# Feature-major k, q and v projections: one 512-column operand instead of three 256-column matmuls, with the halves added when a chunk is emptied

## The chip, the cores and the metric

One Trainium2 chip, of which one core runs the whole program. The metric is the device time of one execution in microseconds (us), from the timed runs of the unchanged kernel and of the changed one.

## What is computed

The reference is one decoder block for 256 tokens of width 2048 in float32. Cut to what matters here:

```python
h = _rms_norm(x, attn_norm)
proj = h @ w_in                      # NSA q, kv, gates | GDN q, k, v | z | a | b | merge gates
o_a = _nsa_mixer(...)                # attention branch
pad = jnp.pad(qkv, ((0, 0), (3, 0), (0, 0)))
conv = sum(conv_w[i] * pad[:, i:i + S_] for i in range(4))
conv = jax.nn.silu(conv)             # then q, k, v of the gated delta rule
o_b = _gated_delta_chunked(...)
x = x + (sigmoid(m_a) * (o_a @ w_branch_a) + sigmoid(m_b) * (o_b @ w_branch_b)) @ w_out
x = x + SwiGLU(_rms_norm(x, ffn_norm))
```

The change touches the product of `h` with the 6144 columns of `w_in` that give q, k and v of the gated delta rule, and the convolution that reads them.

## The kernel before, in words

Every large product is computed from split operands: a float32 number is written as a high part (rounded to the PE's float32r format) and a low part (the remainder), and a product is the sum high·high + high·low + low·high. Activations are split once and kept in SBUF (`hT_hi`, `hT_lo`: the normalised input, transposed, 16 k-tiles of 128 features by 256 tokens). Weights are streamed: `load_pair` (lines 99 to 111) loads two k-tiles by 512 columns with one DMA on SP's queue into `raw`, ScalarE (ACT) makes the high part `whi` (line 107), VectorE (DVE) makes the low part `wlo` (line 108). There are four `raw` buffers and three each of `whi` and `wlo`.

There are two kinds of chunk, each 512 weight columns wide and eight pairs of k-tiles long. A token-major chunk (`chunk_tok`, lines 113 to 128) holds the activations as the stationary operand and moves the 512 weight columns: three matmuls of 512 columns for each k-tile and each half of the tokens (lines 122 to 124), into two PSUM banks. A feature-major chunk (`chunk_feat`, lines 130 to 146) holds 128 of the weight columns as the stationary operand and moves the 256 tokens: for each of 16 k-tiles and each of four column blocks `s` it issues three matmuls of 256 columns (lines 141 to 143), and two column blocks share one PSUM bank, so that the chunk fills two banks. The pool `psm` has four banks with the tag `mm`, so that a chunk of either kind can begin while the one before it is being emptied.

The gated delta rule goes over four groups of four heads (`gdn_group`). Each group runs the k, the q and the v chunk feature-major and then the gate chunk z token-major; after the first two groups a merge-gate chunk follows, and two more come after the fourth. So there are 12 feature-major chunks. When one ends, `conv_silu` (lines 645 to 657) empties it: for each column block ScalarE scales PSUM by the last filter tap (line 651) and VectorE adds the other three taps, reading PSUM three times (line 654). What follows for a group (norms, the products of k with k and q, the inverse of a triangular block matrix, the recurrence, the output norm) is cut into small steps in a queue of side tasks, and two steps are recorded after each pair of k-tiles of the running chunk. The inverse is a serial chain on VectorE (lines 786 and 789, 31 rounds) followed by two round trips through DRAM (`ud<-xl`, `U<-ud`) to the matmuls at line 805. The last steps of the last group are recorded when the first two chunks of the product with `w_branch_b` have come as far as they can without them (`run_pair`).

That is the recorded order. The order in which each engine runs its instructions is then set when the program is built, by a scheduler that may move independent instructions past each other; on the chip each engine takes its list in order.

## Time and profile before

| what | value |
|---|---|
| timed runs (3) | median 1974.73 us, 1974.52 to 1977.64 |
| span of the profiled execution, first to last instruction | 1971.1 us (its whole time is not listed apart; the median of the timed runs is 3.6 us above the span) |
| TensorE (PE) | 99% of the span busy, 10485 matmuls |
| VectorE / ScalarE | 59% / 47% busy |
| DMA | 367 MB, 186 GB/s on average |
| stage of the gated delta rule, where the change lies | about 518 to 1085 us of the span |

How to read it: times are microseconds from the first instruction unless marked ns. A matmul's record lasts from its issue to its modelled end, and the next one begins before it ends, so the pace of the PE is the distance between the starts, not the length of a record. PEld is the weight load that goes with each matmul. The granted clock of the PE is 1.00 at 2.4 GHz and 0.50 at 1.2 GHz. A side matmul in plain float32 shows as two records. A releaser is what ended an engine's wait.

### The profile page before, as it was taken

The numbers are of one execution on the slowest core, as the hardware profiler recorded it, in microseconds if no ns is written. First come the engines' busy times: TensorE is split into PE (matmuls) and PEld (weight loads), VectorE is DVE, ScalarE is ACT, GpSimd is POOL, SyncE is SP. The second block draws the span as 40 slices with busy tenths as digits, with TensorE's granted clock in tenths as the row PEclk, the third lists the DMA queues.
The fourth block names the chain that finished last, engine by engine and source line by source line (L and its number), as shares of the span: only waits on it lengthen the run. The fifth ranks groups of instructions, "written<-read, shape, count | busy, mean of one in ns | idle before, by whom it ended". The sixth has DMA issues, their size and how long they took to land.

```text
span 1971.1 us, 27260 instructions
## 1 busy us (share of the span) xinstructions
PE 1946.4 (99%) x10485; PEld 1651.0 (84%) x10485; DVE 1155.0 (59%) x1715; ACT 928.4 (47%) x1377; POOL 54.1 (3%) x97
## 2 busy tenths in 40 slices
PE   8999999999999999999999999999999999999999
PEld 6878877876998998999987788888888888888887
DVE  5555766655468587687774665554455444544443
ACT  5434555555454554654543544444444444443333
POOL 0001000001000000100100000000000000000000
PEclk9999999999999999999999999999999999999999
DMA  8566545546767566566574965666666666656663
GB/s 231 170 183 193 161 129 162 170 149 200 217 173 203 169 178 198 158 193 166 153 200 157 333 201 183 191 192 183 191 191 186 191 191 191 191 185 201 201 202 130
DMA packets 207605, 367.04 MB, mean 186 GB/s; under 512 B 25473, under 2 KB 34546, under 8 KB 207090
## 3 DMA queue, kind: packets, MB, share of 16 engines
q1 hardware_dynamic: 207442, 365.28, 62.1%
q8 instruction: 82, 1.34, 0.3%
q14 instruction: 49, 0.40, 0.1%
q10 hardware_dynamic: 32, 0.01, 0.0%
HBM read 355.76 MB, written 9.45 MB: 185 GB/s over the span
## 4 chain that ended last, share of the span: by engine, by line
PE 96%; DMA 2%; DVE 1%; ACT 0%; SPq 0%; issue 0%; POOL 0%; ACTq 0%; POOLq 0%; DVEq 0%
PE mm L123 25%; PE mm L124 24%; PE mm L122 24%; PE mm L141 4%; PE mm L143 4%; PE mm L142 4%; PE sd L183 1%; PE sd L668 1%; PE sd L448 1%; PE sd L561 1%; DMA Q<-grow_d 1%; PE sd L748 1%; DMA raw<-in_w_branch_b_dram 1%; PE sd L567 1%; PE sd L568 0%; PE sd L267 0%
## 5 line engine op out<-in xcount | busy, mean ns | idle before, releaser
L108 DVE TENSOR_TENSOR wlo<-raw,whi 128x1024 fp32r<-128x1024 f32 x632 | 773.7, 1225 | 658.5 <-ACT whi L107 656.1
L107 ACT ACTIVATE whi<-raw 128x1024 fp32r<-128x1024 f32 x632 | 669.7, 1060 | 804.5 <-PE mm L124 674.4
L123 PE MATMUL mm<-wlo,hT_hi 128*128 128x512 f32 x704 | 276.7, 393 | 0.0
L124 PE MATMUL mm<-whi,hT_lo 128*128 128x512 f32 x704 | 276.5, 393 | 0.0
L124 PE MATMUL mm<-whi,h2T_lo 128*128 128x512 f32 x704 | 274.0, 389 | 0.0
L123 PE MATMUL mm<-wlo,h2T_hi 128*128 128x512 f32 x704 | 273.9, 389 | 0.0
L122 PE MATMUL mm<-whi,hT_hi 128*128 128x512 f32 x704 | 260.2, 393 | 0.0
L122 PE MATMUL mm<-whi,h2T_hi 128*128 128x512 f32 x704 | 249.9, 390 | 0.0
L143 PE MATMUL mm<-hT_hi,wlo 128*128 128x256 f32 x768 | 218.4, 285 | 0.0
L141 PE MATMUL mm<-hT_hi,whi 128*128 128x256 f32 x768 | 218.4, 285 | 0.0
L142 PE MATMUL mm<-hT_lo,whi 128*128 128x256 f32 x768 | 218.3, 284 | 0.0
L124 PEld LDWEIGHTS mm<-whi,hT_lo 128*128 128x128 f32 x704 | 132.3, 188 | 27.7 <-issue 1.1
L123 PEld LDWEIGHTS mm<-wlo,hT_hi 128*128 128x128 f32 x704 | 132.3, 188 | 27.5 <-issue 1.1
L124 PEld LDWEIGHTS mm<-whi,h2T_lo 128*128 128x128 f32 x704 | 132.2, 188 | 27.5
L122 PEld LDWEIGHTS mm<-whi,h2T_hi 128*128 128x128 f32 x704 | 132.2, 188 | 27.1
L123 PEld LDWEIGHTS mm<-wlo,h2T_hi 128*128 128x128 f32 x704 | 132.2, 188 | 27.0
L122 PEld LDWEIGHTS mm<-whi,hT_hi 128*128 128x128 f32 x704 | 132.1, 188 | 26.3 <-issue 0.2
L141 PEld LDWEIGHTS mm<-hT_hi,whi 128*128 128x128 f32 x768 | 147.2, 192 | 0.6
L142 PEld LDWEIGHTS mm<-hT_lo,whi 128*128 128x128 f32 x768 | 147.2, 192 | 0.2
L143 PEld LDWEIGHTS mm<-hT_hi,wlo 128*128 128x128 f32 x768 | 146.9, 192 | 0.4
L123 PE MATMUL mm<-wlo,act 128*128 128x512 f32 x352 | 138.5, 393 | 0.0
L124 PE MATMUL mm<-whi,act 128*128 128x512 f32 x352 | 138.4, 393 | 0.0
(288 smaller groups left out, 2247.7 us busy)
## 6 DMA issues: line engine op xcount, KB each, us to landing
raw<-in_w_in_dram SPq DMA_DIRECT2D x272, 512.0 KB, 3.7
raw<-in_w_gate_dram SPq DMA_DIRECT2D x88, 512.0 KB, 4.4
raw<-in_w_up_dram SPq DMA_DIRECT2D x88, 512.0 KB, 3.7
raw<-in_w_down_dram SPq DMA_DIRECT2D x88, 512.0 KB, 4.7
raw<-in_w_branch_a_dram SPq DMA_DIRECT2D x32, 512.0 KB, 4.7
raw<-in_w_branch_b_dram SPq DMA_DIRECT2D x32, 512.0 KB, 4.9
raw<-in_w_out_dram SPq DMA_DIRECT2D x32, 512.0 KB, 4.7
wc<-in_w_cmp_dram SPq DMA_DIRECT2D x16, 256.0 KB, 4.2
```

What stands on the lines that cost most here:

```text
L107: nc.scalar.activation(hi[:, :, :width], raw[:, :, :width], AF.Copy)
L108: nc.vector.tensor_tensor(lo[:, :, :width], raw[:, :, :width], hi[:, :, :width].bitcast(F32), ALU.subtract)
L122: nc.tensor.matmul(o, lhsT=sh, rhs=hi[:, j, :width], start=kt == 0, stop=False)
L123: nc.tensor.matmul(o, lhsT=sh, rhs=lo[:, j, :width], start=False, stop=False)
L124: nc.tensor.matmul(o, lhsT=sl, rhs=hi[:, j, :width], start=False, stop=kt == kts - 1)
L141: nc.tensor.matmul(o, lhsT=hi[:, j, ws], rhs=xh[:, kt, :], start=first, stop=False, skip_group_check=True)
L142: nc.tensor.matmul(o, lhsT=hi[:, j, ws], rhs=xl[:, kt, :], start=False, stop=False, skip_group_check=True)
L143: nc.tensor.matmul(o, lhsT=lo[:, j, ws], rhs=xh[:, kt, :], start=False, stop=last, skip_group_check=True)
L183: nc.tensor.transpose(pt[:, i * P : (i + 1) * P], s4, ident)
L448: nc.tensor.matmul(pc[:60, :P], lhsT=kp[:, l0 + l, :], rhs=wc[:, l, :], start=l0 + l == 0, stop=l0 + l == 31)
L561: nc.tensor.transpose(pt[:n, r * P : (r + 1) * P], pb[:, r, c0 : c0 + n], ident)
L567: nc.tensor.matmul(po, lhsT=wh, rhs=ph[:n], start=i == 0, stop=False)
```

## The change

The moving operand of a feature-major chunk becomes one access of 512 columns, the 256 tokens of the high part and then the 256 of the low part. For that the two halves of each large activation are put in one tile (`big_pair`: two buffers of the pool `big` instead of four of half the size). One matmul of 512 columns with the weight's high part now gives high·high in the first half of a PSUM bank and high·low in the second half, and one matmul of 256 columns adds low·high to the first half. A column block therefore takes a whole bank, and a chunk takes all four. When it is emptied, ScalarE copies the second half of each bank to a new tile `xs` in SBUF, VectorE adds the first half to it, and the convolution reads `xs` instead of PSUM. The other lines of the diff follow from the new tiles, or drop comments.

```diff
-    big = ctx.enter_context(tc.tile_pool(name="big", bufs=4))
+    big = ctx.enter_context(tc.tile_pool(name="big", bufs=2))
...
+    def big_pair(name):
+
+        b = big.tile([P, 2, KD, S], F32R, tag="big", name=nm(name))
+        return b, b[:, 0], b[:, 1]
...
-    def chunk_feat(w, c0, evac, xh, xl):
-        ps = [psm.tile([P, 512], F32, tag="mm", name=nm("mm")) for _ in range(2)]
+    def chunk_feat(w, c0, evac, xhl):
+
+        ps = [psm.tile([P, 512], F32, tag="mm", name=nm("mm")) for _ in range(4)]
...
+                first, last = kt == 0, kt == KD - 1
                 for s in range(4):
-                    o = ps[s // 2][:, (s % 2) * S : (s % 2 + 1) * S]
                     ws = slice(s * P, (s + 1) * P)
-                    first = kt == 0 and s % 2 == 0
-                    last = kt == KD - 1 and s % 2 == 1
-                    nc.tensor.matmul(o, lhsT=hi[:, j, ws], rhs=xh[:, kt, :], start=first, stop=False, skip_group_check=True)
-                    nc.tensor.matmul(o, lhsT=hi[:, j, ws], rhs=xl[:, kt, :], start=False, stop=False, skip_group_check=True)
-                    nc.tensor.matmul(o, lhsT=lo[:, j, ws], rhs=xh[:, kt, :], start=False, stop=last, skip_group_check=True)
+                    nc.tensor.matmul(
+                        ps[s].rearrange("p (q c) -> p q c", q=2), lhsT=hi[:, j, ws], rhs=xhl[:, :, kt, :],
+                        start=first, stop=False, skip_group_check=True,
+                    )
+                    nc.tensor.matmul(
+                        ps[s][:, :S], lhsT=lo[:, j, ws], rhs=xhl[:, 0, kt, :], start=False, stop=last, skip_group_check=True
+                    )
...
         ca = gdn.tile([P, 4, S], F32, tag="ca", name=nm("ca"), bufs=2)
+        xs = gdn.tile([P, 4, S], F32, tag="xs", name=nm("xs"), bufs=1)
         for s in range(4):
-            src = ps[s // 2][:, (s % 2) * S : (s % 2 + 1) * S]
+            nc.scalar.activation(xs[:, s, :], ps[s][:, S:], AF.Copy)
+            nc.vector.tensor_tensor(xs[:, s, :], ps[s][:, :S], xs[:, s, :], ALU.add)
+        for s in range(4):
+            src = xs[:, s, :]
             a = ca[:, s, :]
             nc.scalar.activation(a, src, AF.Copy, scale=conv_col(3, base + s))
```

The built programs are the same on every engine up to the first feature-major chunk, and from within the product with `w_branch_b` on. Between them the scheduler has set another order. Three places show it. Line numbers of the changed kernel are higher by two to six than those of the kernel before; `mm` is a PSUM bank of a chunk, `ca` the convolution's result.

The first turn from a k chunk to a q chunk (group 0) on ScalarE. Before:

```order
L107 ACTIVATE whi_4732<-raw_4730 128x1024
L107 ACTIVATE whi_4770<-raw_4768 128x1024
L651 ACTIVATE ca_4686<-mm_4413,cw_425 128x256
L107 ACTIVATE whi_4800<-raw_4798 128x1024
L651 ACTIVATE ca_4686<-mm_4414,cw_425 128x256
L651 ACTIVATE ca_4686<-mm_4413,cw_425 128x256
L107 ACTIVATE whi_4830<-raw_4828 128x1024
```

and now:

```order
L109 ACTIVATE whi_4678<-raw_4676 128x1024
L109 ACTIVATE whi_4708<-raw_4706 128x1024
L652 ACTIVATE xs_4622<-mm_4410 128x256
L652 ACTIVATE xs_4622<-mm_4411 128x256
L652 ACTIVATE xs_4622<-mm_4412 128x256
L109 ACTIVATE whi_4730<-raw_4728 128x1024
L652 ACTIVATE xs_4622<-mm_4413 128x256
L657 ACTIVATE ca_4621<-xs_4622,cw_423 128x256 x4
```

Two conversions for the next chunk (4678 and 4708) still stand ahead of the emptying; three of the four copies come before the third conversion.

The same turn on VectorE, now:

```order
L110 TENSOR_TENSOR wlo_4679<-raw_4676,whi_4678 128x1024
L110 TENSOR_TENSOR wlo_4709<-raw_4706,whi_4708 128x1024
L653 TENSOR_TENSOR xs_4622<-mm_4410,xs_4622 128x256
L653 TENSOR_TENSOR xs_4622<-mm_4411,xs_4622 128x256
L653 TENSOR_TENSOR xs_4622<-mm_4412,xs_4622 128x256
L110 TENSOR_TENSOR wlo_4731<-raw_4728,whi_4730 128x1024
L653 TENSOR_TENSOR xs_4622<-mm_4413,xs_4622 128x256
L660 SCALAR_TENSOR_TENSOR ca_4621<-xs_4622,cw_423,ca_4621 128x255 x3
```

The additions stand behind the conversion of the second pair of the q chunk, and three of the four ahead of the third pair's. On the PE the q chunk opens with the eight matmuls on its first bank for both of these pairs, and only then goes to the second bank. Most of the other q and v chunks open in the same way; at seven of the twelve turns out of a feature-major chunk, side matmuls stand at the boundary as well.

The end of the last group's side tasks, on the PE. `y` is the output of one half of the tokens, whose four transposes (line 668, now 674) end the work of that half; `mm` here are banks of the `w_branch_b` chunks. Before, around the first half's `y`:

```order
L124 MATMUL mm_10357<-whi_10450,oTB_lo_4368 128x512
L122 MATMUL mm_10356<-whi_10450,oTB_hi_4367 128x512
L123 MATMUL mm_10356<-wlo_10451,oTB_hi_4367 128x512
L668 MATMUL sd_9904<-ident,y_9899 128x128 x4
L903 MATMUL sd_9929<-ssb_9861,kq_8562 128x128 x4
L911 MATMUL sd_9939<-ssb_9861,eR_8789 128x128 x4
L124 MATMUL mm_10356<-whi_10450,oTB_lo_4368 128x512
```

and now:

```order
L899 MATMUL sd_9217<-w_9215,ksc_8394 128x128 x4
L904 MATMUL sd_9224<-w_9215,Q_8270 128x128 x4
L674 MATMUL sd_9265<-ident,y_9260 128x128
L909 MATMUL sd_9290<-ssb_9222,kq_8082 128x128 x4
L917 MATMUL sd_9300<-ssb_9222,eR_8271 128x128 x4
L674 MATMUL sd_9265<-ident,y_9260 128x128 x3
L923 MATMUL sd_9305<-vb_9028,U 128x128 x4
L124 MATMUL mm_9606<-whi_9834,oTB_4365 128x512
L125 MATMUL mm_9606<-wlo_9835,oTB_4365 128x512
L124 MATMUL mm_9716<-whi_9906,oTB_4365 128x512
L125 MATMUL mm_9716<-wlo_9907,oTB_4365 128x512
L928 MATMUL sd_9300<-w_9310,Q_8270 128x128 x4
```

Before, 39 matmuls of 512 columns stand between the matmul that `y` is made from (line 898) and its transposes. Now none stands there; 14 stand between line 928 and the second half's transposes, where before none did.

## Rows read from the trace of the kernel before

**Rows 1.** The page, its head and part 1: span, busy time and share by engine.
```profile
span 1971.1 us, 27260 instructions
PE 1946.4 (99%) x10485; PEld 1651.0 (84%) x10485; DVE 1155.0 (59%) x1715; ACT 928.4 (47%) x1377; POOL 54.1 (3%) x97
```
**Rows 2.** Busy time by window: stretch, its length, busy by engine, granted clock, DMA share, GB/s.
```profile
530.00:560.00 30.00, 30.00 (x253) 30.00 (x252) 17.81 (x24) 16.82 (x33) 1.56 (x1) 1.00 0.63 178
...
740.00:770.00 30.00, 30.00 (x145) 25.28 (x144) 27.04 (x56) 13.85 (x15) 0.00 (x0) 1.00 0.70 197
```
**Rows 3.** Waits of the PE between 500 and 1100 us: total, times, longest.
```profile
PE sd L668 <- DVE y L871: 3.8, 2, 3.5
PE mm L122 <- ACT oTB_hi L877: 0.8, 1, 0.8
PE mm L123 <- DVE wlo L108: 0.6, 1, 0.6
PE sd L805 <- DMA U<-ud: 0.5, 2, 0.4
```
**Rows 4.** Timeline of the PE in a k chunk, 82 matmuls in turn: start, length.
```profile
524.35 0.28 PE L141 MATMUL mm<-hT_hi,whi 128*128 128x256 f32 x1
...
534.07 0.28 PE L141 MATMUL mm<-hT_hi,whi 128*128 128x256 f32 x1
```
**Rows 5.** Timeline of the PE in a token-major chunk, 14 matmuls in turn.
```profile
1260.04 0.39 PE L123 MATMUL mm<-wlo,h2T_hi 128*128 128x512 f32 x1
...
1261.17 0.61 PE L122 MATMUL mm<-whi,h2T_hi 128*128 128x512 f32 x2
...
1262.99 0.39 PE L124 MATMUL mm<-whi,h2T_lo 128*128 128x512 f32 x1
```
**Rows 6.** Groups by line on ScalarE and VectorE: count, busy, mean ns of one, idle before.
```profile
L108 DVE TENSOR_TENSOR wlo<-raw,whi 128x1024 fp32r<-128x1024 f32 x632 | 773.7, 1225 | 658.5 <-ACT whi L107 656.1
L107 ACT ACTIVATE whi<-raw 128x1024 fp32r<-128x1024 f32 x632 | 669.7, 1060 | 804.5 <-PE mm L124 674.4 <-PE mm L142 73.3 <-issue 31.1
...
L663 ACT ACTIVATE sq<-sd 128x128 f32<-128x128 f32 x96 | 25.3, 282 | 7.4 <-PE sd L922 3.7 <-PE sd L668 2.4 <-PE sd L898 0.9
...
L651 ACT ACTIVATE ca<-mm,cw 128x256 f32<-128x256 f32 x48 | 22.7, 472 | 25.2 <-DVE ca L654 14.2 <-PE mm L143 10.9
...
L604 ACT ACTIVATE stg<-mm 128x512 f32<-128x512 f32 x24 | 14.4, 600 | 11.8 <-PE mm L124 11.1
...
L761 DVE TENSOR_TENSOR Q<-sd,Q 128x128 f32<-128x128 f32 x32 | 8.9, 278 | 0.0
...
L990 DVE TENSOR_TENSOR gb<-mm,gb 128x512 f32<-128x512 f32 x8 | 5.4, 681 | 0.0
```
**Rows 7.** Timeline at a turn from k to q: a bank's last matmul, ScalarE's first reading.
```profile
540.79 0.28 PE L143 MATMUL mm<-hT_hi,wlo 128*128 128x256 f32 x1
...
541.12 0.47 ACT L651 ACTIVATE ca<-mm,cw 128x256 f32<-128x256 f32 x1 [1.22 <-PE mm L143]
```
**Rows 8.** Timeline of the PE, end of the last group's side tasks.
```profile
1060.55 1.06 PE L898 MATMUL sd<-w,Q 128*128 128x128 f32 x8
...
1070.34 0.60 PE L668 MATMUL sd<-ident,y 128*128 128x128 f32 x4
...
1078.51 1.05 PE L922 MATMUL sd<-w,Q 128*128 128x128 f32 x8
1083.08 1.16 PE L668 MATMUL sd<-ident,y 128*128 128x128 f32 x4 [3.52 <-DVE y L871]
1085.02 0.80 PE L122 MATMUL mm<-whi,oTB_hi 128*128 128x512 f32 x1 [0.78 <-ACT oTB_hi L877]
```
**Rows 9.** Busy time by window after that wait, columns as in rows 2.
```profile
1084.00:1086.00 2.00, 1.22 (x3) 0.83 (x3) 0.75 (x1) 0.69 (x1) 0.00 (x0) 0.50 0.38 66
...
1090.00:1092.00 2.00, 2.00 (x10) 1.68 (x9) 1.15 (x1) 1.22 (x1) 0.00 (x0) 0.97 1.01 304
```
**Rows 10.** Timeline of VectorE at the last group's inverse: its end, then the block matrix back from DRAM.
```profile
1019.61 0.42 DVE L789 TENSOR_REDUCE xl<-pr 128x8 f32<-128x256 f32 x1
...
1027.88 1.25 DVE L800 STREAM_TRANSPOSE X<-U 128x1024 f32<-128x1024 f32 x1 [3.19 <-DMA U<-ud]
```

More of the change, by code (lines that the diff above doesn't have):

```diff
@@ L91, in nm @@
         return f"{s}_{uid[0]}"
-    def big_tile(name, dt=F32):
-        return big.tile([P, KD, S], dt, tag="big", name=nm(name))
+    def big_pair(name):
+        b = big.tile([P, 2, KD, S], F32R, tag="big", name=nm(name))
+        return b, b[:, 0], b[:, 1]
     def sps():
@@ L234, in tile_hybrid_block @@
     nsa = scr.__enter__()
-    hT_hi = big_tile("hT_hi", F32R)
-    hT_lo = big_tile("hT_lo", F32R)
-    xin = big.tile([P, NT, D], F32, tag="big", name="xin")
+    hT, hT_hi, hT_lo = big_pair("hT")
+    xin = big.tile([P, 2, NT, D], F32, tag="big", name="xin")[:, 0]
     for t in range(NT):
@@ L358, in narrow @@
         yield
-    oTA_hi = big_tile("oTA_hi", F32R)
-    oTA_lo = big_tile("oTA_lo", F32R)
+    _, oTA_hi, oTA_lo = big_pair("oTA")
     kTh = nsa.tile([P, G, 528], F32R, name="kTh")
@@ L627, in tile_hybrid_block @@
         run(g)
-    oTB_hi = big_tile("oTB_hi", F32R)
-    oTB_lo = big_tile("oTB_lo", F32R)
+    _, oTB_hi, oTB_lo = big_pair("oTB")
     scr = tc.tile_pool(name="gdn", bufs=1)
@@ L962, in evac_z @@
                 side.append(gdn_fin(st, hg))
-        run(chunk_feat(w_in, C_QKV + 2048 + hg * 512, evac_k, hT_hi, hT_lo), 2)
-        run(chunk_feat(w_in, C_QKV + hg * 512, evac_q, hT_hi, hT_lo), 2)
-        run(chunk_feat(w_in, C_QKV + 4096 + hg * 512, evac_v, hT_hi, hT_lo), 2)
+        run(chunk_feat(w_in, C_QKV + 2048 + hg * 512, evac_k, hT), 2)
+        run(chunk_feat(w_in, C_QKV + hg * 512, evac_q, hT), 2)
+        run(chunk_feat(w_in, C_QKV + 4096 + hg * 512, evac_v, hT), 2)
         run(chunk_tok(w_in, C_Z + hg * 512, 512, KD, stat_h, evac_z), 2)
@@ L974, in tile_hybrid_block @@
         chunk_m("mB_d", c, 2)
-    mixT_hi = big_tile("mixT_hi", F32R)
-    mixT_lo = big_tile("mixT_lo", F32R)
+    _, mixT_hi, mixT_lo = big_pair("mixT")
     def evac_brB(c):
@@ L1009, in tile_hybrid_block @@
         nc.sync.dma_start(x2[:, t, :], x[t * P : (t + 1) * P, :])
-    h2T_hi = big_tile("h2T_hi", F32R)
-    h2T_lo = big_tile("h2T_lo", F32R)
+    _, h2T_hi, h2T_lo = big_pair("h2T")
     ss2 = fin.tile([P, NT, 4], F32, name="ss2")
@@ L1030, in tile_hybrid_block @@
     act = [[], []]
+    act0 = big_pair("act0")[1:]
     for q in range(2):
@@ L1037, in tile_hybrid_block @@
             else:
-                act[q].append(big_tile(f"act{q}{i}", F32R))
+                act[q].append(act0[q])
     rs2 = fin.tile([P, NT], F32, name="rs2")
```

## The prediction, made blind

> **What bounds the kernel now.** I read the page's head first: the PE is busy for 99% of a span of 1971.1 us [rows 1], so only PE time counts unless a change makes it wait. The windows of the gated delta stage say the same of the place of the change: in a stretch of 30 us of a k chunk the PE is busy for all 30 at a granted clock of 1.00, VectorE for 17.8 and ScalarE for 16.8; in a stretch where the inverse runs, VectorE comes to 27.0, with the PE still at 30 [rows 2]. The list of the PE's waits shows how little is lost: 3.8 us for `y` at the end of a group's side tasks, 0.8 us for `oTB_hi`, 0.6 us for a low weight part, 0.5 us for the block matrix `U` [rows 3]. No wait for a PSUM bank is among them: with two of four banks to a chunk, a chunk is emptied behind the next one.
>
> The busy share doesn't tell the pace, since records overlap. It is read from starts. In a k chunk 81 steps lie between 524.35 and 534.07 us, 120.0 ns each [rows 4]. In a token-major chunk 13 steps of 512 columns lie between 1260.04 and 1262.99 us, 226.9 ns each [rows 5]. Twice 120.0 is 240.0, so one matmul of 512 columns is 13.1 ns cheaper than two of 256: at 2.4 GHz the columns alone take 106.7 and 213.3 ns, and some 13 ns more come with each matmul, whatever its width. That is what the change can save.
>
> **Matmuls.** For each k-tile and column block three matmuls of 256 columns (360.0 ns) become one of 512 and one of 256 (226.9 + 120.0 = 346.9 ns). There are 12 chunks x 16 k-tiles x 4 blocks = 768 of these, and 768 x 13.1 ns = **10.1 us less**, all on the path. No row shows a moving operand read as two separate runs. The bounds are the two rows at hand: as one matmul of 512 (226.9 ns) or as two of 256 (240.0 ns, which saves nothing). I take the first, since the instruction has the output shape, the bank and the columns of rows 5, and only its read address jumps once.
>
> Here the Trainium skill speaks against the change. On the page "TensorE: Matmul & The Clock Gate", section "Back-to-back issue gap", a warm matmul is said to cost N/2.4 ns plus 2.5 ns. By that the fixed part would be a fifth of what rows 4 and 5 show, and the saving, an estimate by that page, 768 x 2.5 ns = 1.9 us. The trace disagrees: both widths carry 13 ns here, so the sum goes by the rows.
>
> **Turning from one chunk to the next.** A feature-major chunk now holds all four banks, so the next chunk's first matmul waits until the first bank has been copied and added. No row before shows this wait; I build it from rows. Let 0 be the moment at which the PE would go on. The first bank's last matmul starts at 120.0 + 3 x 346.9 ns before it, at -1.16 us. ScalarE can begin 0.33 us after such a start (540.79 to 541.12) [rows 7]: -0.83. A copy of 256 columns lies between 282 ns for 128 and 600 ns for 512; in proportion 388 ns, and at most the 472 ns of the scaled one [rows 6]: the copy ends at -0.44. The addition on VectorE lies between 278 and 681 ns, in proportion 412 ns [rows 6]. It stands behind the low part of the next chunk's second pair, whose buffers come free one pair (8 x 346.9 ns) before 0: released at -2.57, high part 1060 ns, low part 1225 ns [rows 6], done at about -0.25. So the first bank is free at about +0.2 us. The second is ready some 0.4 us later, while the PE has four times 346.9 ns of work on the first, and later banks follow the same way. The 12 convolution steps behind the additions take VectorE over 5 us (they are not new, but they came interleaved with conversions before) and can make one conversion about 0.2 us late. I charge 0.4 us to each of the five bare turns and 0.15 us to each of the seven at which side matmuls stand at the boundary and cover it: 2.0 + 1.0 = **3.0 us more**. The bounds: nothing, since no wait for a bank is in the trace now [rows 3]; and a whole conversion on both engines, 1060 + 1225 ns [rows 6], in front of the emptying.
>
> Per chunk the new copies and additions are 4 x 0.39 us on ScalarE and 4 x 0.41 us on VectorE, 19 and 20 us in all. Apart from the turns I cost them at nothing: the cover is the slack of both engines behind the PE [rows 2]. If that goes, in the stretches with the inverse, the weight parts are late next.
>
> **The end of the last group.** In this trace the side chain runs out of cover only at its last step: `y` 3.52 us late, then `oTB_hi` 0.78 us, 4.3 us together [rows 8]. The first half's `y` cost nothing, because 9 us of `w_branch_b` work stood in front of it (1060.55 to 1070.34) [rows 8]. In the new order the first half's `y` follows at once, so it waits the same 3.5 us. The second has 14 x 226.9 ns = 3.2 us in front and waits about 0.4 us. `oTB_hi` stays at 0.8 us and the steps between add 0.2 us: 4.9 us, **0.6 us more**. Bounds: 3.5 us less, if both `y` are covered, and 3.5 us more, if neither is. After the idle time the granted clock fell to 0.50 and was back at 0.97 some 6 us later [rows 9]. I expect the same dip once and charge nothing for it.
>
> **The inverse.** It is a serial chain on VectorE and does not get faster when the PE does. The scheduler has therefore pulled later chunk work ahead of line 805 (now 811), so that the PE comes to it at nearly the same time as before. In the last group the chain ended at 1020.03 us and `U` came back from DRAM at 1027.88 us, VectorE having waited 3.2 us for it [rows 10]. I charge **0.7 us more** waiting for `U` over the four groups; bounds none and 3.2 us.
>
> The new tile layout changes no instruction elsewhere, and nothing is added on SP's or POOL's queue; four large buffers became two of twice the size with the same lifetimes. I cost these at nothing. The DMA share of 0.63 to 0.70 [rows 2] leaves room for weights that are wanted 3.6% sooner.
>
> **Sum.** -10.1 + 3.0 + 0.6 + 0.7 = -5.8 us on the profiled span of 1971.1, so 1965.3 us. The median of the timed runs, 1974.73, lies 3.6 us above that span, and I keep the distance: **1968.9 us**. A difference of 0.2% (3.95 us) is about what a measurement of this kernel can tell from none.
>
> **Rivals.** *The turns are hidden.* The scheduler stacks the first bank's work for two pairs and side matmuls at the boundaries; if the copies and additions are a little quicker than I scale them, only the ends are paid. -10.1 + 0.6 = -9.5 us: 1965.2 us. For it: 0.2 us is all that was missing in my count of a bare turn. Against it: every engine must be punctual twelve times.
>
> *The turns eat the gain.* If each of the 12 costs 0.75 us, from a late conversion or side work on an in-order queue ahead of a copy, that is 9.0 us: -10.1 + 9.0 + 1.3 = +0.2 us, 1974.9 us, no change. For it: around the inverse VectorE is at 27.0 of 30 us [rows 2], so there is little room to catch up.
>
> *Slower: the emptying stands behind a whole conversion.* Its place is the first bank at each turn. If the next chunk's second pair is converted late, copy and addition queue behind 1.06 us on ScalarE and 1.23 us on VectorE [rows 6]. Then a bare turn costs 0.4 + 2.3 = 2.7 us and a covered one some 0.9 us less, 1.8: 5 x 2.7 + 7 x 1.8 = 26.1 us, and -10.1 + 26.1 + 1.3 = +17.3 us, 1992.0 us. It decides from a mean turn of (10.1 - 1.3) / 12 = 0.73 us on. Against it: the conversions in the new order stand ahead of the emptying, with their buffers free 2.6 us before the turn.
>
> *The saving isn't there.* If the two runs of the operand stream as two matmuls of 256 columns would, 240.0 ns, the 10.1 us fall away and 3.0 + 1.3 us remain: 1979.0 us, slower. Rows 4 and 5 speak against it only so far as both have one run. By the page's 2.5 ns named above, an estimate, it would be 1977.1 us.
>
> **How the numbers follow.** Chances: forecast 0.52 (its own range 1966 to 1972), hidden turns 0.15, eaten gain 0.20, behind a conversion 0.06, no saving 0.07. The two slower cases and the outer part of the eaten gain are left out of the range: 1965.0 to 1976.5 us. Faster means below 1970.8: all of the hidden case and three quarters of the forecast, 0.15 + 0.39 = 0.54. Slower means above 1978.7: 0.06 + 0.05 + 0.02 = 0.13. The same: 0.33.
>
> **What the changed profile would show.** Right: starts 227 ns apart after a 512-column matmul of a feature-major chunk and 120 ns after a 256-column one; a new wait of the PE for `xs`, or an idle start at the first matmul of q, v and z chunks, of a few tenths of a us each; two waits for `y` in the last group, one near 3.5 us; the same clock dip. Wrong: 240 ns in place of 227; waits for `xs` of more than 0.7 us on average; waits for `wlo` inside the k, q and v chunks; a wait for `U` of several us; or a PE idle for longer at the end of the last group, with a longer stretch at 0.50.

## The result, and the profile after

The changed kernel takes 1986.82 us (median of 5 runs, 1986.60 to 1988.29); the kernel before, run beside it, 1974.73 us (5 runs, 1972.49 to 1977.64). The ratio is 1.0066 with a 95% interval of 1.0054 to 1.0078: **13 us slower**, where 5.8 us faster was forecast and 1976.5 us was the upper end of the range. The profiled execution took 1986.82 us with a span of 1985.1 us, 14.0 us more than the span before [rows 1].

The page's head and part 1, after:

```profile
span 1985.1 us, 25807 instructions
PE 1946.0 (98%) x9717; PEld 1610.9 (81%) x9717; DVE 1171.2 (59%) x1763; ACT 940.7 (47%) x1425; POOL 54.5 (3%) x97
```

The PE is busy for as long as before although 768 matmuls are gone, and the span is longer: time has gone into idleness. The waits of the PE between 500 and 1115 us, after (total us, times, longest), against [rows 3]:

```profile
PE mm L124 <- DVE gb L995: 4.1, 1, 4.1
PE mm L142 <- ACT whi L109: 4.0, 2, 2.3
PE sd L674 <- DVE y L877: 3.7, 2, 3.5
PE mm L146 <- DVE wlo L110: 3.0, 3, 1.5
PE mm L124 <- DVE xs L653: 2.0, 2, 1.6
PE sd L811 <- DMA U<-ud: 1.0, 1, 1.0
PE mm L125 <- DVE wlo L110: 0.9, 1, 0.9
PE mm L124 <- ACT oTB L883: 0.8, 1, 0.8
PE mm L142 <- DVE xs L653: 0.6, 1, 0.6
```

The waits for `xs` are the turns (2.6 us, with those too short for this list 2.9). New beside them are waits for weight parts, `whi` and `wlo`, in the middle of chunks (8.1 us with the short ones), and one of 4.1 us for `gb`, a tile of the emptying of the `w_branch_b` chunks.

**Where the time went.** Both programs run the same PE instructions up to the first feature-major matmul and again from a point inside the `w_branch_b` product on (817.9 us before the last matmul ends in both traces). Between the two points, in us, summed over the PE's starts in each trace (the last three columns are experiments below):

| | before | changed | e4 | e15 | e17 |
|---|---|---|---|---|---|
| length of this stretch | 630.2 | 642.4 | 633.3 | 625.6 | 628.8 |
| feature-major matmuls, without idle time | 282.5 | 278.8 | 275.5 | 283.1 | 275.0 |
| PE idle | 6.1 | 20.4 | 14.7 | 4.2 | 11.4 |
| - at turns (`xs`) | 0 | 2.9 | 2.0 | 0 | 1.9 |
| - for `whi` and `wlo` | 0.7 | 8.1 | 1.3 | 0 | 1.2 |
| - for `y` and `oTB` | 4.6 | 4.5 | 7.7 | 0.6 | 2.2 |
| - for `gb` | 0.2 | 4.1 | 1.6 | 3.6 | 4.0 |
| granted clock at 0.50 for | 6.8 | 10.2 | 6.8 | 3.4 | 6.8 |

The first two columns differ by 12.2 us: 14.3 more idle, 3.7 less in the feature-major matmuls (5 less without the slow clock that fell on some of them), 1.6 more in the others. The stretches at 0.50 are 3.4 us longer, and half of such a stretch is lost. The start of the first feature-major matmul, up to which nothing differs, lies between 518.1 and 521.1 us in all traces of this study; that is noise. Eight of these nineteen traces have a stretch at 0.50 of 3.4 or 6.8 us some 470 us into the span, and eleven have none, though every engine's list is the same up to there.

**The matmul pair.** The first k chunk shows its pace undisturbed. Timeline of the PE, its first and its last matmul after:

```profile
520.31 0.62 PE L142 MATMUL mm<-hT,whi 128*128 128x512 f32 x2
...
542.70 0.28 PE L146 MATMUL mm<-hT,wlo 128*128 128x256 f32 x1
```

64 pairs take 542.70 + 0.12 - 520.31 = 22.5 us, 352 ns each; the median steps of all chunks are 233 ns after a 512-column matmul and 117 ns after a 256-column one, 350 together. Before, the triple took 360. So 8 to 10 ns are saved 768 times, 6 to 8 us, and e4, whose feature-major chunks saw no slow clock, has 282.5 - 275.5 = 7.0 us.

**The late conversions.** Timeline of VectorE in the first half of group 1's v chunk:

```profile
705.57 0.42 DVE L653 TENSOR_TENSOR xs<-mm,xs 128x256 f32<-128x256 f32 x1
708.71 0.88 DVE L714 TENSOR_SCALAR Q<-Q,gcum 128x128 f32<-128x128 f32 x4 [2.71 <-DMA Q<-grow_d]
709.50 1.23 DVE L110 TENSOR_TENSOR wlo<-raw,whi 128x1024 fp32r<-128x1024 f32 x1
```

The loads it waits for, on SP's queue, and the PE shortly behind:

```profile
702.29 0.89 SPq L705 DMA_DIRECT2D Q<-grow_d  x2
...
710.77 0.74 PE L146 MATMUL mm<-hT,wlo 128*128 128x256 f32 x4 [1.53 <-DVE wlo L110]
```

VectorE stands idle for 2.71 us with the remaining convolution steps and a weight conversion behind this wait in its list. What it waits for is the decay matrix `Q` of group 2, whose k chunk begins at 778 us: the scheduler has put this work here as soon as a buffer comes free. The rows land 6.4 us after their issue at 702.29. The low part is converted at 709.50 and the PE has run dry. The same block, for group 3, stands in group 2's v chunk (waits of 1.7 and 1.2 us at 845.5 and 847.9 us). These three waits are 4.4 of the 8.1 us.

The longest wait, 2.29 us for `whi` at 682.28 in group 1's q chunk, comes from ScalarE's list:

```profile
676.93 0.60 ACT L901 ACTIVATE ssb<-sd 128x512 f32<-128x512 f32 x1 [2.89 <-PE sd L899]
677.90 1.28 ACT L941 ACT_TABLE_LOAD   x1 [0.37 <-DVE ca L660]
...
681.16 2.96 ACT L109 ACTIVATE whi<-raw 128x1024 fp32r<-128x1024 f32 x3
```

ScalarE stands still for a side matmul that the PE reaches late, then for the convolution, and three conversions wait behind both. Nothing in this stretch waits for `Q`.

**The end of the last group.** PE timeline, after, against [rows 8]:

```profile
1084.84 0.30 PE L674 MATMUL sd<-ident,y 128*128 128x128 f32 x1 [3.45 <-DVE y L877]
...
1095.13 1.10 PE L674 MATMUL sd<-ident,y 128*128 128x128 f32 x4 [0.24 <-DVE y L877]
1097.02 0.50 PE L124 MATMUL mm<-whi,oTB 128*128 128x512 f32 x1 [0.78 <-ACT oTB L883]
...
1103.72 0.39 PE L126 MATMUL mm<-whi,oTB 128*128 128x512 f32 x1
1108.19 0.50 PE L124 MATMUL mm<-whi,oTB 128*128 128x512 f32 x1 [4.08 <-DVE gb L995]
```

and on SP's queue and VectorE:

```profile
1096.32 0.35 SPq L1008 DMA_DIRECT2D gain<-in_ffn_norm_dram  x1
...
1097.65 0.68 SPq L991 DMA_DIRECT2D ba<-brA_d  x1
...
1105.70 0.69 DVE L994 TENSOR_TENSOR ba<-ba,ga 128x512 f32<-128x512 f32 x1 [2.86 <-DMA ba<-brA_d]
...
1107.45 0.68 DVE L995 TENSOR_TENSOR gb<-mm,gb 128x512 f32<-128x512 f32 x1
```

The pool for the last stage takes the memory of the group's tiles, so SP's queue stood shut for 13.9 us, until the last `y` had been read; then come the gain, `ga`, `gb` and `ba`, and 11.1 us after the gain's issue the first bank is emptied. Before, the queue stood shut for 7.8 us, and the bank was emptied 9.5 us after the gain's issue. The PE had 30 matmuls as cover for this path, the first eleven at half clock, and waited 0.2 us. Now a weight conversion stands between lines 994 and 995, as many matmuls run at full clock, and the PE waits 4.1 us. In 15 of the 19 traces the end of the span lies 888 to 891 us behind the start of the last `y` transposes (before 1971.1 - 1083.1, after 1985.1 - 1095.1, e4 1975.6 - 1087.7): **in these orders the end follows the last `y`**. The others are e10 and e11 (897 and 892 us) and e5 and e6, where the last `y` comes 45 us and more earlier and the end does not come so much earlier with it. The work behind the last `y` is nearly the same everywhere, so this distance alone doesn't show what makes `y` late.

**The clock.** Windows of the PE behind the wait of 2.29 us for `whi` at 682.28 (columns as in [rows 2]):

```profile
682.00:684.00 2.00, 1.72 (x6) 1.29 (x7) 1.74 (x3) 2.00 (x3) 0.83 (x1) 0.69 0.00 0
684.00:686.00 2.00, 2.00 (x9) 1.81 (x9) 2.00 (x6) 0.12 (x1) 0.00 (x0) 0.50 0.69 175
686.00:688.00 2.00, 2.00 (x12) 1.74 (x12) 0.96 (x2) 1.06 (x1) 0.00 (x0) 0.96 0.94 264
```

The granted clock falls to 0.50 and is back some 3.4 us later. It does so twice more, at 1085.5 and 1109.4 us, behind the waits for `y` and `gb`: three dips where one was expected. No single wait can be charged with a dip, though. In e1, which has the same order on every engine, the wait for `whi` at that place is 2.21 us and no dip follows; nor does one follow its wait of 3.46 us for `y`. Its stretches at 0.50 stand elsewhere and come to 13.7 us against 10.2 here.

### The profile page after: what moved, and what is told of

It is laid out like the page before. It is cut to its first block, busy times and chain, and to the rows that moved or that the text cites. A ratio compares the mean times of both kernels' runs of the same rounds, so it can differ in the third digit from the quotient of the medians.

```text
span 1985.1 us, 25807 instructions
## 1 busy us (share of the span) xinstructions
PE 1946.0 (98%) x9717; PEld 1610.9 (81%) x9717; DVE 1171.2 (59%) x1763; ACT 940.7 (47%) x1425; POOL 54.5 (3%) x97
## 4 chain that ended last, share of the span: by engine, by line
PE 61%; DVE 2%; DMA 1%; ACT 0%; SPq 0%; issue 0%; POOL 0%; ACTq 0%; POOLq 0%; DVEq 0%
PE mm L125 17%; PE mm L124 17%; PE mm L126 17%; PE mm L142 4%; PE mm L146 2%; PE sd L188 1%; DVE ca L660 1%; PE sd L674 1%; DMA Q<-grow_d 1%; DVE wlo L110 1%; PE sd L754 1%; DMA ba<-brA_d 0%; PE sd L917 0%; DMA eR<-grow_d 0%; PE sd L909 0%
## 5 line engine op out<-in xcount | busy, mean ns | idle before, releaser
L125 PE MATMUL mm<-wlo,hT 128*128 128x512 f32 x704 | 277.1, 394 | 0.9 <-DVE wlo L110 0.9
L126 PE MATMUL mm<-whi,hT 128*128 128x512 f32 x704 | 276.7, 393 | 0.0
L126 PE MATMUL mm<-whi,h2T 128*128 128x512 f32 x704 | 274.0, 389 | 0.0
L125 PE MATMUL mm<-wlo,h2T 128*128 128x512 f32 x704 | 273.9, 389 | 0.0
L142 PE MATMUL mm<-hT,whi 128*128 128x512 f32 x768 | 263.2, 400 | 4.8 <-ACT whi L109 4.0
L124 PE MATMUL mm<-whi,hT 128*128 128x512 f32 x704 | 261.6, 394 | 2.0 <-DVE xs L653 2.0
L124 PE MATMUL mm<-whi,h2T 128*128 128x512 f32 x704 | 249.9, 390 | 0.0
L146 PE MATMUL mm<-hT,wlo 128*128 128x256 f32 x768 | 198.4, 284 | 3.1 <-DVE wlo L110 3.0
L142 PEld LDWEIGHTS mm<-hT,whi 128*128 128x128 f32 x768 | 141.4, 189 | 35.4 <-ACT whi L109 4.7
L124 PEld LDWEIGHTS mm<-whi,hT 128*128 128x128 f32 x704 | 132.1, 188 | 29.0 <-DVE xs L653 2.7
L126 PEld LDWEIGHTS mm<-whi,hT 128*128 128x128 f32 x704 | 132.3, 188 | 27.7 <-issue 1.1
L126 PEld LDWEIGHTS mm<-whi,h2T 128*128 128x128 f32 x704 | 132.2, 188 | 27.5
L124 PEld LDWEIGHTS mm<-whi,h2T 128*128 128x128 f32 x704 | 132.2, 188 | 27.1
L146 PEld LDWEIGHTS mm<-hT,wlo 128*128 128x128 f32 x768 | 140.4, 190 | 9.4 <-DVE wlo L110 5.0
```

The costliest lines, as they stand in the source:

```text
L124: nc.tensor.matmul(o, lhsT=sh, rhs=hi[:, j, :width], start=kt == 0, stop=False)
L125: nc.tensor.matmul(o, lhsT=sh, rhs=lo[:, j, :width], start=False, stop=False)
L126: nc.tensor.matmul(o, lhsT=sl, rhs=hi[:, j, :width], start=False, stop=kt == kts - 1)
L142: nc.tensor.matmul(ps[s].rearrange("p (q c) -> p q c", q=2), lhsT=hi[:, j, ws], rhs=xhl[:, :, kt, :], start=first, stop=False, skip_group_ ...
L146: nc.tensor.matmul(ps[s][:, :S], lhsT=lo[:, j, ws], rhs=xhl[:, 0, kt, :], start=False, stop=last, skip_group_check=True)
```

## The experiments

Each edit changes what the scheduler sees, and it may set a new order for all engines; only e1 has the changed kernel's order to the last instruction, and e7 up to the end of the last group. Ratios are to the kernel before, run beside them.

| run | edit | median us | ratio, 95% interval |
|---|---|---|---|
| e1 | changed; operand in one run of memory | 1986.76 | 1.0067, 1.0053 to 1.0081 |
| e2 | before; with the new emptying | 1981.03 | 1.0039, 1.0026 to 1.0051 |
| e3 | changed; matmuls not fused | 1987.56 | 1.0071, 1.0058 to 1.0084 |
| e4 | changed; preparation held back | 1977.32 | 1.0019, 1.0011 to 1.0028 |
| e5 | before; chain cut | 1974.82 | 1.0003, 0.9994 to 1.0012 |
| e6 | changed; chain cut | 1970.16 | 0.9985, 0.9976 to 0.9993 |
| e7 | changed; gain loaded later | 1987.36 | 1.0068, 1.0054 to 1.0082 |
| e8 | before; preparation held back | 1974.05 | 1.0001, 0.9992 to 1.0010 |
| e9 | changed; only Q held back | 1980.24 | 1.0037, 1.0024 to 1.0051 |
| e10 | e9; loads on POOL's queue | 1989.00 | 1.0077, 1.0064 to 1.0089 |
| e11 | e9; addition on POOL | 1983.31 | 1.0048, 1.0035 to 1.0060 |
| e12 | e4; shorter chain | 1979.64 | 1.0027, 1.0019 to 1.0036 |
| e13 | e8; shorter chain | 1969.92 | 0.9982, 0.9973 to 0.9991 |
| e14 | changed; shorter chain | 1986.17 | 1.0064, 1.0051 to 1.0076 |
| e15 | before; shorter chain | 1969.98 | 0.9979, 0.9970 to 0.9987 |
| e16 | e4; additions first | 1985.45 | 1.0056, 1.0042 to 1.0069 |
| e17 | e12; additions first | 1972.48 | 0.9992, 0.9983 to 1.0001 |

### The pieces of the change: e1, e2, e3

e1 stores the halves side by side for each k-tile:

```diff
-        b = big.tile([P, 2, KD, S], F32R, tag="big", name=nm(name))
-        return b, b[:, 0], b[:, 1]
+        b = big.tile([P, KD, 2, S], F32R, tag="big", name=nm(name))
+        return b, b[:, :, 0], b[:, :, 1]
```

> The changed kernel with its activation halves stored as [tile, half, token], so that the 512 moving columns of a feature-major matmul are one run of memory; the instruction order of every engine is the same as in the changed kernel. In the changed kernel the 512-column matmul takes 233 ns from start to start and the 256-column one behind it 117 ns, 350 together, where the rows of before promised 226.9 + 120.0 = 346.9. Theory A (the jump in the read address costs some ns): the pair falls to about 347 ns or less, and the time by 768 x 3 ns = 2.4 us, to some 1984.5 us. Theory B (the jump costs nothing, the pair is what it is because matmuls of two widths alternate): the pair stays at 350 ns and the time within 1 us of 1986.8.

The steps are again 233 and 117 ns and the time is that of the changed kernel. The jump in the read address costs nothing; theory B holds.

e2 takes the kernel before and gives it the emptying, in `conv_silu`:

```diff
+            nc.scalar.activation(xs[:, s, :], half, AF.Copy)
+            nc.vector.tensor_tensor(xs[:, s, :], half, xs[:, s, :], ALU.max)
```

> The kernel before (three matmuls of 256 columns, two banks to a chunk), with the emptying of the change put in: ScalarE copies each column block to the new tile xs, VectorE passes over it once more (a maximum of the block with its own copy, which changes no value and costs what the addition costs), the convolution reads xs. Theory A (what the change lost it lost because its new emptying work stands ahead of weight conversions in the in-order lists of ScalarE and VectorE): conversions come late here too, waits of the PE for whi and wlo inside q and v chunks of 4 us or more, time 1978 to 1984 us. Theory B (the loss comes from holding all four banks, or from the faster PE): with two banks nothing waits, 1974 to 1977 us.

The time is 0.39% longer (7.7 us by the ratio), inside theory A's range, but not for its reason. The PE's waits in e2:

```profile
PE mm L122 <- DVE gb L995: 4.0, 1, 4.0
PE sd L673 <- DVE y L876: 3.9, 3, 3.5
PE mm L122 <- ACT oTB_hi L882: 0.8, 1, 0.8
PE mm L123 <- DVE wlo L108: 0.7, 2, 0.4
PE mm L143 <- DVE wlo L108: 0.6, 2, 0.3
```

No conversion is late and no turn waits. The last `y` comes 569.0 us after the first feature-major matmul instead of 564.5 (up to 1.7 us of this is a dip of the clock ahead of it), and the wait for `gb` follows. So the emptying, with the order that comes with it, lengthens the chain of side tasks.

e3 keeps banks and emptying, and takes the matmul apart:

```diff
-                    nc.tensor.matmul(
-                        ps[s].rearrange("p (q c) -> p q c", q=2), lhsT=hi[:, j, ws], rhs=xhl[:, :, kt, :],
-                        start=first, stop=False, skip_group_check=True,
-                    )
+                    nc.tensor.matmul(ps[s][:, :S], lhsT=hi[:, j, ws], rhs=xhl[:, 0, kt, :], start=first, stop=False, skip_group_check=True)
+                    nc.tensor.matmul(ps[s][:, S:], lhsT=hi[:, j, ws], rhs=xhl[:, 1, kt, :], start=False, stop=False, skip_group_check=True)
```

> The changed kernel with its banks and its emptying, but each 512-column matmul taken apart again into two of 256 columns. Theory A (lists put emptying and side steps ahead of conversions): the waits stay as in the changed kernel or shrink a little because the PE is slower by 10 ns a triple, so 1983 to 1990 us. Theory B (the four held banks and the turns cost what the change lost, and the fusing gains its 5 to 8 us): 1992 to 1995 us. Theory C (the faster pace of the PE makes the conversions late): waits for whi and wlo nearly gone, about 1980 us.

1987.56 us, by the number theory A, but its waits are others than A named:

```profile
PE mm L124 <- DVE xs L655: 5.4, 3, 2.4
PE sd L676 <- DVE y L879: 5.3, 2, 3.5
PE mm L142 <- DVE xs L655: 1.2, 1, 1.2
...
PE mm L142 <- ACT whi L109: 0.6, 1, 0.6
PE mm L125 <- DVE wlo L110: 0.6, 1, 0.6
```

Four banks bring 6.7 us at the turns. The conversions are in time again: theory C has its mechanism here and misses the time. Read as steps, the emptying costs some 7 us, the four banks 6.5 more, and the fusing nothing either way: what it saves on its matmuls and at the turns it loses to late conversions and `gb`.

### The late conversions: e4, e8, e9

e4 queues the early preparation behind a conversion of its own time (an edge that sets VectorE's order only; `last_lo` is the subtraction that `load_pair` recorded last):

```diff
+                with tc.issue_after(last_lo[0]):
                     nc.vector.tensor_scalar(st.N[:, i, :], st.N[:, i, :], gc, 0.0, ALU.subtract, ALU.max)
                     nc.vector.tensor_scalar(st.Q[:, i, :], st.Q[:, i, :], gc, 0.0, ALU.subtract, ALU.min)
```

> The changed kernel, with the preparation of the next group's decay factors on VectorE (the subtractions on N and Q, line 713 and 714) queued behind the weight conversion that was recorded last before them, so that the scheduler can no longer put them two chunks earlier, where VectorE in the changed kernel stood idle for 2.7 us in each of two places until the rows of Q came from DRAM. Theory A (these side steps, placed too early, make the conversions late): the waits at 710.8, 714.0, 845.5 and 847.9 us (4.5 us together) go, 1981 to 1984 us. Theory B (the conversions are late because the emptying and convolution load VectorE, whatever stands among them): others come in their place, 1986 to 1989 us.

1977.32 us: 9.5 us of the 13 are back, more than theory A gave. The waits for `whi` and `wlo` inside q and v chunks are gone but for 0.1 us, the one at 682.28 too, although nothing there waited for `Q`: in ScalarE's new list a conversion stands ahead of the steps that made it late. So a part of the gain comes from the new order and not from the block itself. What is left:

```profile
PE sd L677 <- DVE y L881: 6.9, 2, 3.5
PE mm L127 <- DVE xs L656: 2.0, 1, 2.0
PE mm L127 <- DVE gb L999: 1.6, 1, 1.6
PE mm L128 <- DVE wlo L112: 1.2, 2, 0.6
```

e8 is the control, the same edit in the kernel before.

> The kernel before, with the same holding back of the next group's preparation as in the run on the changed kernel that gained 9.5 us. Theory A (it cured late conversions, which the kernel before doesn't have): no gain, 1973 to 1978 us. Theory B (it is a better order for either kernel): 5 us or more faster, below 1969 us.

No gain: the kernel before has the same early block, but its conversions are far enough ahead. VectorE's waits for its rows in the kernel before, between 510 and 1100 us:

```profile
DVE Q L708 <- DMA Q<-grow_d: 6.4, 4, 3.0
```

The list of the PE's waits [rows 3] shows only 0.6 us for a low part over the same stretch. Theory A.

e9 holds back the second of the two lines alone.

> The changed kernel, with only the subtractions on Q of the next group (line 714, the ones that wait for rows from DRAM) queued behind the weight conversion recorded last before them; those on N stay where the scheduler puts them. Theory A (the wait for the rows of Q in VectorE's list is what makes the conversions late): the waits for whi and wlo at 711, 714, 846 and 848 us go as in the run that held back both, and the chain of side tasks starts no later, so the waits for y are smaller than the 6.9 us there: 1973 to 1977 us. Theory B (holding back N did it, by moving 8 more instructions): waits for whi and wlo of over 3 us stay, 1980 to 1985 us.

The same waits go, so holding back `Q` is enough and `N` isn't needed, as theory A says. The time isn't theory A's: 1980.24 us lies at the lower end of theory B's range. The waits for `y` are 6.9 us as in e4, where A expected fewer, and those for `xs` rise to 4.5.

### The end of the last group: e7, e10

e7 moves the gain's load behind the loop over the chunks.

```diff
-    nc.sync.dma_start(gain2, ffn_norm.partition_broadcast(P).rearrange("p o d -> p (o d)"))
     for g in br:
         run(g)
+    nc.sync.dma_start(gain2, ffn_norm.partition_broadcast(P).rearrange("p o d -> p (o d)"))
```

> The changed kernel, with the load of the second norm's gain (1 MB, line 1008) issued after the product with w_branch_b and not ahead of the loads of its stored partners ga, gb and ba; the order of all engines up to the end of the last group is that of the changed kernel. Theory A (the 4.1 us wait for gb is the path from the last y over the queue of SP: the gain, then ga, gb, ba): the wait falls to some 1 to 2 us, time 1983 to 1985 us. Theory B (the wait for gb comes from elsewhere, as from late weights): unchanged, 1986 to 1988 us.

The wait for `gb` is gone and the time is not: a wait of 2.4 us for a high weight part stands in its place. Its conversion stands on ScalarE behind the sigmoid of `ga`, for whose load ScalarE sits idle for 3.4 us; the weights themselves were loaded before the queue was shut. Neither theory: the order of the loads isn't it. e10 starts from e9 and gives the four loads to POOL's queue (`nc.gpsimd.dma_start` for `nc.sync.dma_start`).

> The same with the loads of the gain and of ga, gb and ba issued from POOL's queue, so that the weight loads on SP's queue no longer stand behind loads that wait until the last y has been read. Theory A (after the last y the PE waits because SP's queue was shut until then): 1 to 4 us faster than the run before it in this list. Theory B (only the landing of gb and ba themselves counts): within 1 us of it, or slower if POOL's queue is slower to issue.

Worse than e9 by 8.8 us. The loads still start only behind the last `y`, and `gb` is now waited for 5.5 us instead of 1.6. About as much comes from the clock: in the trace 20.5 us of the stage are at 0.50, against 10.2 in e9, and half of the difference is lost. Theory A falls; how much of the loss is the queue's is left open.

### The chain of side tasks: e5, e6, e12 to e15

e5 and e6 cut it:

```diff
-            nc.sync.dma_start(U[bs, :, bs], ud.rearrange("(h b) c i -> b c h i", b=4)[b])
+            nc.sync.dma_start(U[bs, :, bs], ld.rearrange("(h b) c i -> b c h i", b=4)[b])
```

> The kernel before with the serial chain of the inverse cut: the block matrix U is read back from the DRAM tile that the inverse starts from (ld), which is there some 55 us earlier, and not from the one that it ends in (ud). All 31 rounds on VectorE still run and are still written out; what is left out is that anything uses them, so the result is another. Theory A (the chain of side tasks from group to group, not the PE's work, ends last at the end of the last group): the 4.3 us of waits for y and oTB there and the slow clock behind them go, 1966 to 1969 us. Theory B (the PE's own work bounds everything): within 1 us of 1974.

> The changed kernel with the same cut (the inverse is computed, but nothing uses it). Theory A (in the changed kernel the emptying and the late conversions lengthen the chain of side tasks, and the chain ends last; the saving on the PE is there, but the PE waits it away): without the chain the change is faster than the kernel before with the same cut, by 3 to 7 us, so 1960 to 1966 us. Theory B (the loss is in the turns and in the emptying itself, whatever the chain does): still slower than the kernel before with the same cut, by 5 us or more, 1972 us or above.

What they leave out is the use of the inverse, so their results are others. e5 missed theory A's range, and its time is theory B's: the waits at the last group's end went, and the dip with them, but others for weights (5.6 us in all) and for earlier `y` (2.9 us) came, and the time stayed. So the chain isn't the only thing that holds the kernel before at its time. e6 missed its range by 4 us, but the sign is theory A's: with the chain out of the way the changed kernel is faster than the other one (1970.16 against 1974.82), by 4.7 us, with 4.3 us of turns still in it.

e12 to e15 shorten the chain without leaving anything out. In `gdn_fin` the transposes of the first half's `y` go behind the second half's matmuls:

```diff
-        yield from gdn_out(st, hg, 0, po)
+        first = gdn_out(st, hg, 0, po)
+        next(first)
+        yield
...
+        yield from first
         yield from gdn_out(st, hg, 1, po)
```

> The kernel before with the transposes moved alone. Theory A (chain): 1967 to 1971 us, the waits for y at the end of the last group below 1 us. Theory B: 1973 to 1975 us.

> The kernel before with both edits. Theory A (the chain sets the end there too, by little: 4.3 us of waits for y and oTB): 1967 to 1972 us, and the changed kernel with both edits is at most level with it or faster by up to 4 us, since its matmuls take 7 us less and its turns 2 to 4 us more. Theory B (the chain isn't the bound): 1973 to 1975 us, and the changed kernel with both edits stays 3 us or more behind.

> The changed kernel with the transposes moved, and the preparation not held back. If the late conversions (8 us of waits in the q and z chunks) cost by themselves, they stay: 1977 to 1984 us. If they only cost because they delay the chain: below 1975 us.

> The changed kernel with the preparation held back, and in addition the four transposes of the first half's y moved behind the matmuls of the second half, which don't depend on them. Theory A (the chain of side tasks sets the end): the last y is done several us earlier, the waits for y (6.9 us with the preparation held back alone) fall below 4 us, time 1969 to 1974 us. Theory B (the chain isn't what bounds it): within 1.5 us of 1977.3.

The kernel before gains 4.1 us in e15 (0.21%) and as much in e13, by theory A: in this order the chain set its end, and these two are the fastest kernels of the study. In e15 the last `y` comes 5.8 us earlier from the first feature-major matmul on; a wait of 3.6 us for `gb` takes back a part, and 1.7 us of the gain is the shorter dip. The changed kernel gains nothing: e14 is above both of its ranges, and e12 is 2.3 us above e4, where theory B allowed 1.5. It is 9.7 us behind e13, where e13's theory A had expected it level or ahead. The PE's waits in e12:

```profile
PE mm L127 <- DVE xs L656: 6.7, 3, 3.0
PE mm L127 <- DVE gb L1002: 4.1, 1, 4.1
PE mm L127 <- ACT oTB L887: 2.2, 2, 1.4
```

No wait for `y` is left, but the turns have grown from 2.0 to 7.6 us (with the short waits). In e14 they are 12.3 us, and the late conversions 1.5: there the turns took the place of both other waits.

### The turns: e11, e16, e17

What a long turn is made of shows in the changed kernel, from v to z in group 0. VectorE:

```profile
593.25 1.22 DVE L110 TENSOR_TENSOR wlo<-raw,whi 128x1024 fp32r<-128x1024 f32 x1
594.39 0.17 DVE L795 TENSOR_REDUCE xl<-pr 128x8 f32<-128x24 f32 x1
594.47 0.75 DVE L653 TENSOR_TENSOR xs<-mm,xs 128x256 f32<-128x256 f32 x2
```

and the PE:

```profile
593.07 0.27 PE L146 MATMUL mm<-hT,wlo 128*128 128x256 f32 x1
594.94 0.50 PE L124 MATMUL mm<-whi,hT 128*128 128x512 f32 x1 [1.60 <-DVE xs L653]
```

A whole conversion of 1.22 us and rounds of the inverse stand ahead of the additions. e11 starts from e9 and takes the addition off VectorE:

```diff
-            nc.vector.tensor_tensor(xs[:, s, :], ps[s][:, :S], xs[:, s, :], ALU.add)
+            nc.scalar.activation(ca[:, s, :], ps[s][:, :S], AF.Copy)
+            nc.gpsimd.tensor_tensor(xs[:, s, :], ca[:, s, :], xs[:, s, :], ALU.add)
```

> The changed kernel with Q held back, and the addition of the halves taken from VectorE to POOL: ScalarE copies both halves of a bank to SBUF and POOL adds them there, so that a bank is free after two copies on ScalarE. Theory A (the additions on VectorE lengthen the turns, and through the inverse the chain of side tasks): the waits at the turns out of feature-major chunks (2.0 us in the run with both held back) fall below 1 us, and the time is 1 to 4 us less than with Q held back alone. Theory B (they cost nothing there; POOL's addition makes the convolution later): the same or up to 4 us slower.

No wait for `xs` is left, but 6.0 us for `wlo` and 3.2 us for `whi` have come, five of them of about 1 us each in token-major chunks. Theory B by the time. e16 (from e4) and e17 (from e12) queue the low parts of the next chunk's second to fifth pair behind the last addition, with the same `tc.issue_after`.

> The changed kernel with the preparation held back, and the low-part conversions of the second to fifth pair of the chunk that follows a feature-major chunk queued on VectorE behind that chunk's last addition. Theory A (the waits for xs at the turns come from additions behind whole conversions): the waits for xs fall below 1.5 us, the low parts come in time, 1973 to 1976 us. Theory B (with four banks held the turn costs this whatever stands first: what xs gains, wlo loses): waits for wlo of 2 us or more come in their place, 1977 to 1982 us.

> The same with the shorter chain of side tasks as well. Theory A: the 7.6 us of waits for xs fall below 2.5 us, 1972 to 1975 us. Theory B: waits for wlo come in their place, 1977 to 1982 us. In either case it is not expected to beat the kernel before with the shorter chain (1970.0 us), because one turn is left to pay for at each feature-major chunk, 12 in all.

```profile
PE mm L132 <- DVE wlo L116: 7.8, 4, 2.9
PE sd L682 <- DVE y L886: 6.9, 2, 3.5
```

These are e16's longest waits: what `xs` gains `wlo` loses, theory B. Its time, 1985.45 us, is above both ranges. Against e4 the PE idles only 3.1 us more in the trace; the stretches at 0.50 in the stage come to 20.5 us instead of 6.8, which is worth 6.8 us. In e17, with the shorter chain, only 1.9 us for `xs` and 1.2 us for `wlo` are left, theory A, and its 1972.48 us can't be told from the kernel before. Against e15, which has the shorter chain without the change, it is still 2.5 us behind. So the same rule helps in one order and hurts in the other, and which turn is long hangs on the whole order. That is as far as the runs settle it.

## Why the prediction was wrong, step by step

Between the forecast of 5.8 us less and the 12.2 us more of the table lie 18.0 us: 6.4 in the matmuls, 7.4 in waits for weight parts, 3.9 in the wait for `gb` and 1.6 in the other instructions, less some 1.3 by which the forecast waits came out shorter.

- **The step that failed**: "Apart from the turns I cost them at nothing: the cover is the slack of both engines behind the PE". The shares were right (VectorE is at 59% now as before), but a share is no cover on an engine that takes its list in order. A block that waits for a DMA stands in both lists; in the old order conversions were far enough ahead to pass over it, in the new one they weren't. The term put at nothing came to 8.1 us of waits for weight parts, against 0.7 before. Of these 4.4 us stand behind the block, 2.3 behind ScalarE's wait for a late side matmul, and 1.3 behind convolution steps on VectorE (at 743 and 921 us). With the block held back nearly all of them go, in the time 9.5 of 13 us (e4) or 6.6 (e9), and the kernel before gains nothing by it (e8). Each of these runs has a new order as a whole, so this isn't the price of the block alone. The text named late weight parts as what would be late next and as a sign of being wrong, but no term or rival priced a wait on another step ahead of a conversion.
- **The matmuls**: forecast 10.1 us, measured 3.7 in this run, 5 without the slow clock, and 7.0 in e4. The steps of rows 4 and 5, each in a chunk of one width, don't add up where the widths alternate: 233 + 117 instead of 226.9 + 120.0 at the median, with 352 ns in the first k chunk. That the operand has two runs is not why (e1); what else the 3 to 5 ns of a pair are stays open. By the 2.5 ns in the Trainium skill's page "TensorE: Matmul & The Clock Gate", section "Back-to-back issue gap", it would have been 1.9 us, an estimate. The page gives this figure for an isolated matmul, which the prediction left out; here they come in a stream, each with a weight load, and one matmul fewer at the same columns was worth 13 ns by rows 4 and 5 and 8 to 10 ns as measured.
- **The turns**: forecast 3.0 us, measured 2.9, but not spread as charged: 1.6 us at one bare turn (v to z), four between 0.1 and 0.6, the others nothing. At the long one the mechanism is that of the rival "the emptying stands behind a whole conversion", which was given 0.06. Other orders of the same work have 7 to 12 us here (e3, e12, e14), so the agreement is partly luck.
- **The end of the last group**: the waits for `y` and `oTB` came as worked out, 3.45, 0.24 and 0.78 us against 3.5, 0.4 and 0.8. What follows on the last `y` was missed: the shut queue, the loads and `gb`, 3.9 us more.
- **The inverse**: 0.7 us more forecast for `U`, 0.45 us found. But the deeper point beside it was passed over: the kernel before already waited for the end of this chain, so PE time saved ahead of it could only be cashed if the chain became shorter too. e2 shows that it became longer with the emptying alone, e15 that a shorter chain is worth 4.1 us to the kernel before; e5, with the chain cut and no gain, shows that other waits stand close behind.
- **The clock**: "the same dip once" was wrong: three dips of 3.4 us against one of 6.8, some 1.7 us. Where they fall differs between executions of the same order (e1).

## What to carry to other kernels

On engines that run their lists in order, ask of each new or moved instruction what stands ahead of it that may wait for a DMA or another engine, and how far ahead the work is that must not be late; a busy share doesn't answer that. Find out what the kernel waits for at the end of a stage before crediting saved work inside it: here the span was the last `y` plus 888 to 891 us in 15 traces. A pace read from chunks of one shape isn't the pace of a mixture: here it promised 347 ns and the pair took 350 to 352.

## What the runs showed of the hardware

A 512-column and a 256-column matmul in alternation took 233 and 117 ns from start to start, where each among its own kind took 227 and 120; a moving operand of two runs of 256 columns cost the same as one of 512. The rows of `Q` landed 6.4 us after their issue. Loads issued from POOL's queue at the end of the last group left the PE waiting 5.5 us for `gb`, against 1.6 us with the same loads on SP's queue (e10, e9). A wait of the PE of 2.3 us was followed by 3.4 us at a granted clock of 0.50; the wait of 2.2 us at the same place of the same order in e1 was not, nor one of 3.0 us in e12 (at 726 us).
